# GLA heads of a two-layer trunk on one Trainium2 core: modulation steps moved behind the reads of two PSUM banks

## The chip, the cores and the metric

The program runs on 1 core of one Trainium2 chip. The metric is the time of one execution on the device, in microseconds, as the median of several runs. The core has five engines that take their instructions in order, each from a queue of its own: TensorE (PE; its weight loads are listed as PEld), VectorE (DVE), ScalarE (ACT), GpSimd (POOL) and SyncE (SP), which here only issues DMA transfers. Engines wait for one another through semaphores. Matmuls write to PSUM, eight banks called b0 to b7; everything else lies in SBUF, in slots of a fixed size.

## The reference

A trunk of two layers on one sequence of 1024 tokens with 1024 features, in float32. Each layer norms its input, modulates it by a shift and a scale that are computed from a conditioning vector c, runs a token mixer, adds the result with a gate, and does the same with a SwiGLU channel mixer. Layer 0 mixes by forgetting attention, layer 1 by gated linear attention (GLA). The parts that matter here:

```python
mod = c_act @ ada_w[i] + ada_b[i]                       # c_act = silu(c): 1024 x 6144 per layer
sh1, sc1, g1, sh2, sc2, g2 = jnp.split(mod, N_MOD, axis=-1)
...
q, k, v, r, a_lr = jnp.split(h @ w_in, [...])           # GLA: 4 heads, q and k 128 wide, v and r 256
log_alpha = log_sigmoid(a_lr @ w_a2 + b_a) / 16
b = cumsum of log_alpha within a chunk
q_in, k_in = q * exp(b), k * exp(-b)
A = tril(q_in @ k_in^T);  o_intra = A @ v
k_dec = k * exp(b_last - b);  kv = k_dec^T @ v          # state update per chunk
o = o_intra + q_in @ state;  o = norm(o) * g_o * silu(r)
```

## The kernel before

Float32 products are made of three matmuls each, on a high and a low part of both operands (mm3, lines 305 to 307; the parts are made by split, lines 174 and 175: ScalarE casts the high part, VectorE subtracts it to get the low one). The program goes through layer 0, then GLA, then the second layer's FFN. Projections read the modulated input h1 as 8 feature tiles of 128 by 1024 tokens, in two halves of 512 tokens; one half of one projection (proj) is 24 matmuls of 512 columns into one PSUM bank.

GLA runs head by head. For a head h, gate_body makes the decay factors by exponentials (ei, b16, t2). head_front then projects k (bank gk, two halves) and q (bank gqp, two halves). VectorE reads each gk bank twice, into gy = k times ei (from which kih and kil are split) and into t2 = k times its decay; it reads each gqp bank twice, into q times ei and q times b16, both split (gq..h, gq..l). head_back makes the masked products (at, L2177, ahl), the state updates (kd, kv, S_t) and the output (go), and is woven with r_proj, the projection of r (gr). gv_body projects v for the next head. The projections of gk, gqp, gr and gv take their banks in turn from one ring of three, so that a projection can start only when the bank that was used three turns before it has been read. In head 2 the first r projection takes the bank of gk's second half.

Between these parts the program also computes the modulation of layer 1. That is work for VectorE and SyncE: ada_w is read in steps of 32 * 2 rows (ada_load, L442: four transfers of 64 KB, into one of two raw buffers in turn), and a step is two instructions on VectorE (L503 or L505), each of which multiplies 256 columns by a value of c and adds them to an accumulator. A step's load can be issued only when the step two before it has been computed, since it goes into the same buffer. In names of tiles, the accumulator and the first raw buffer lie in one slot (an instruction reads ad_s only: first buffer) and the second in another (an instruction reads a second ad_s, after c: second buffer).

The call ada1(5.1) gives these steps time at fixed places of the program: the class Pace adds 5.1 to an account and runs the next pieces of a step as long as the account is not negative; a step is worth 3.6 there (ADA_A and ADA_B). The calls stand in gv_body, r_proj and head_front. The order in which the program is written is not the order on an engine: a scheduler takes the instructions in program order as its priority and places them by a timeline of its own, so that an instruction written later can come earlier on its engine.

## Time and profile before

| what | value |
|---|---|
| median of 3 runs | 2354.34 us (2350.84 to 2356.11) |
| the profiled execution | 2352.71 us |
| its span, first to last instruction | 2351.0 us |
| mean granted clock of TensorE | 0.996 |
| GLA heads, about | 1290 to 1640 us of the span |

The profile is one execution, recorded by the hardware. Its page gives busy time per engine, the chain of work that ended last and the costliest groups of instructions. In a row of the order of time the columns are: start in us from the span's start, duration in us, engine, line of the kernel, operation, output<-inputs by name (numbers left out), sizes, count, and in brackets how long the engine had been idle before and what ended that. Durations of matmuls overlap, since they are pipelined: the distance between two starts tells how fast TensorE goes. In the list of waits a row is: engine, tile and line that waited, what it waited for, us in total, how many times, the longest.

### The profile page before, as it was taken

The page shows a single profiled execution, that of the slowest core. Times are in us where ns is not written, and L with a number is a line of the kernel's source. Part 1 is how long each engine was busy: PE and PEld are TensorE (multiplying, and loading weights), DVE is VectorE, ACT ScalarE, POOL GpSimd, SP SyncE. Part 2 cuts the span into 40 slices and gives each one's busy share as a digit, 9 for nine tenths or more (in the row PEclk, how much of TensorE's full clock was granted, in tenths as well). Part 3 has the DMA queues.
Part 4 walks back from the last instruction along what each step waited for, and adds up shares of the span by engine and source line. Part 5 has one row for each costly group of instructions (what it writes and reads, how often), then busy time and mean ns, then how long its engine had stood idle before and what let it go on. Part 6 is the DMA issues. An engine that isn't in the chain of part 4 may idle for free. (4 is left out here: it accounts for less than half of the span.)

```text
span 2351.0 us, 35555 instructions
## 1 busy us (share of the span) xinstructions
PE 2327.1 (99%) x12168; PEld 1981.4 (84%) x12168; DVE 1780.7 (76%) x2947; ACT 1121.9 (48%) x2166; POOL 1139.3 (48%) x1005
## 2 busy tenths in 40 slices
PE   8999999999999999999999999999999999999999
PEld 7888888888888888888888898898888888888888
DVE  6578787886688888886787665568787777876887
ACT  6666566665453333344334644345544333345236
POOL 1334444533355656664563431335456666664651
PEclk8999999999999999999999999999999999999999
DMA  8423343332435545458774443455434544458674
GB/s 263 149 85 109 104 122 95 122 126 99 129 101 178 188 157 172 156 180 305 261 255 156 143 127 90 140 179 170 140 111 158 176 149 159 139 189 299 238 262 142
DMA packets 349614, 383.38 MB, mean 163 GB/s; under 512 B 25372, under 2 KB 286648, under 8 KB 349432
## 3 DMA queue, kind: packets, MB, share of 16 engines
q1 hardware_dynamic: 349432, 381.11, 49.3%
q8 instruction: 96, 1.57, 0.3%
q14 instruction: 86, 0.70, 0.1%
HBM read 279.76 MB, written 101.25 MB: 162 GB/s over the span
## 5 line engine op out<-in xcount | busy, mean ns | idle before, releaser
L174 ACT CAST o_s<-xv_s 128x512 fp32r<-128x512 f32 (+1 forms) x392 | 236.4, 610 | 340.2 <-PE p_b L307 257.2
L175 DVE TENSOR_TENSOR o_s<-xv_s,o_s 128x512 fp32r<-128x512 f32 (+1 forms) x392 | 336.5, 863 | 43.7 <-ACT o_s L174 43.0
L307 PE MATMUL p_b<-B,o_s 128*128 128x512 f32 x608 | 236.0, 389 | 0.0
L306 PE MATMUL p_b<-B,o_s 128*128 128x512 f32 x608 | 235.9, 389 | 0.0
L305 PE MATMUL p_b<-B,o_s 128*128 128x512 f32 x608 | 235.4, 390 | 0.0
L1293 POOL TENSOR_SCALAR lp_s<-lp_s,st 128x128 f32<-128x128 f32 (+7 forms) x128 | 96.9, 761 | 247.9 <-DVE st L1292 229.0
L940 POOL TENSOR_TENSOR ex_s<-xv_s,xv_s 128x512 f32<-128x512 f32 (+1 forms) x64 | 94.8, 1481 | 239.8 <-DMA xv_s<-in_ffn_w_in_dram 121.9
L305 PE MATMUL p_b<-T,o_s 128*128 128x512 f32 x480 | 186.8, 389 | 0.0
L306 PE MATMUL p_b<-T,o_s 128*128 128x512 f32 x480 | 186.7, 389 | 0.0
L307 PE MATMUL p_b<-T,o_s 128*128 128x512 f32 x480 | 181.2, 389 | 0.0
L307 PEld LDWEIGHTS p_b<-B,o_s 128*128 128x128 f32 x608 | 114.1, 188 | 23.9
L305 PEld LDWEIGHTS p_b<-B,o_s 128*128 128x128 f32 x608 | 114.1, 188 | 23.7 <-DVE x L1659 0.2
L306 PEld LDWEIGHTS p_b<-B,o_s 128*128 128x128 f32 x608 | 114.1, 188 | 23.5
L1291 ACT ACTIVATE lp_s<-lp_s,st 128x128 f32<-128x128 f32 (+7 forms) x128 | 99.3, 776 | 57.9 <-DVE st L1287 56.5
L942 POOL TENSOR_TENSOR xv_s<-ex_s,xv_s 128x512 f32<-128x512 f32 (+1 forms) x64 | 93.8, 1466 | 60.6 <-DVE o_s L175 57.7
L1659 DVE TENSOR_TENSOR ex_s<-ex_s,p_b 128x512 f32<-128x512 f32 x140 | 94.2, 681 | 38.0 <-PE p_b L307 37.8
L174 ACT CAST pt_s<-t_b 128x512 fp32r<-128x512 f32 (+1 forms) x160 | 79.7, 547 | 73.5 <-PE t_b L1313 72.9
L952 POOL TENSOR_TENSOR xv_s<-xv_s,xv_s 128x512 f32<-128x512 f32 x48 | 65.5, 1364 | 92.3 <-issue 50.4
L175 DVE TENSOR_TENSOR pt_s<-t_b,pt_s 128x512 fp32r<-128x512 f32 (+1 forms) x160 | 96.2, 630 | 15.9 <-ACT pt_s L174 15.4
L246 POOL TENSOR_TENSOR w_l_s<-w__s,w_h_s 128x256 fp32r<-128x256 f32 x90 | 69.4, 800 | 77.1 <-ACT w_h_s L242 59.2
L307 PEld LDWEIGHTS p_b<-T,o_s 128*128 128x128 f32 x480 | 90.1, 188 | 18.7
L306 PEld LDWEIGHTS p_b<-T,o_s 128*128 128x128 f32 x480 | 90.1, 188 | 18.7
(1527 smaller groups left out, 7409.5 us busy)
## 6 DMA issues: line engine op xcount, KB each, us to landing
xv_s<-in_ffn_w_in_dram SPq DMA_DIRECT2D x176, 256.0 KB, 3.3
hid_B<-x SPq DMA_DIRECT2D x66, 512.0 KB, 2.8
ad_s<-in_ada_w_dram SPq DMA_DIRECT2D x384, 64.0 KB, 2.4
hid_T<-x SPq DMA_DIRECT2D x44, 512.0 KB, 2.9
xv_s<-in_ffn_w_out_dram SPq DMA_DIRECT2D x88, 256.0 KB, 3.5
ada_s<-in_ada_w_dram SPq DMA_DIRECT2D x96, 128.0 KB, 2.8
T2o<-hid_T SPq DMA_DIRECT2D x22, 512.0 KB, 7.5
T1o<-hid_T SPq DMA_DIRECT2D x22, 512.0 KB, 6.2
```

The lines of the kernel that those rows point to most:

```text
L174: nc.scalar.copy(hi, src)
L175: nc.vector.tensor_sub(lo, src, hi.bitcast(F32))
L246: (nc.gpsimd if i < 3 else nc.vector).tensor_sub(lo[:, cs], rw[:, cs], hi[:, cs].bitcast(F32))
L305: nc.tensor.matmul(ps, ah, bh, start=start, stop=False, skip_group_check=chain)
L306: nc.tensor.matmul(ps, ah, bl, start=False, stop=False, skip_group_check=chain)
L307: nc.tensor.matmul(ps, al, bh, start=False, stop=stop, skip_group_check=chain)
L940: nc.gpsimd.tensor_add(s1, a21, a22)
L942: nc.gpsimd.tensor_sub(a11, s1, a11)
L952: nc.gpsimd.tensor_sub(r[A12], r[A12], r[A11])
L1291: nc.scalar.activation(lp, lp, AF.Exp, bias=mcur, scale=-1.0, accum_out=st[:, qi, 2:3])
L1293: nc.gpsimd.tensor_scalar(lp, lp, st[:, qi, 3:4], 1.0, op0=ALU.mult, op1=ALU.mult)
L1659: nc.vector.tensor_add(d, d if src is None else dest(G, src), ps)
```

## The change

In head_front two calls ada1(5.1) move. The one that stood right behind the projection of gk comes after VectorE's two multiplications that read gk's bank and after the split of the first product; the one that stood right behind the projection of gqp comes after both multiplications that read gqp's bank and after their splits. Each stands in a loop over two halves, so it is four calls a head.

```diff
             ps = pj([P, HALF], F32, f"gk{h}{hf}")
             with ExitStack() if h else tc.issue_after(z_last):
                 run(proj(ps, wk, h1, hf))
-            ada1(5.1)
             next(sums, None)
             y = yv()
             nc.vector.tensor_mul(y, ps, ei[:, cs])
             nc.vector.tensor_mul(t2[:, cs], ps, t2[:, cs])
             split(kin.hi[:, cs], kin.lo[:, cs], y)
+            ada1(5.1)
...
             ps = pj([P, HALF], F32, f"gqp{h}{hf}")
             run(proj(ps, wq, h1, hf))
-            ada1(5.1)
             next(sums, None)
             for t, f in zip(qt, (ei, b16)):
                 y = yv()
                 nc.vector.scalar_tensor_tensor(y, ps, QS, f[:, cs], op0=ALU.mult, op1=ALU.mult)
                 split(t.hi[:, cs], t.lo[:, cs], y)
+            ada1(5.1)
```

Lines 2135 to 2153 thereby move up by one: the reads of gk's bank are L2137 and L2138 before and L2136 and L2137 in the change, the reads of gqp's L2153 and L2152.

VectorE, head 2, second half of gk. The rows are a piece of the difference; gk_b_33 is that bank, ad_s_12831 alone the first raw buffer, ad_s_12832 the second:

```order
 L505 SCALAR_TENSOR_TENSOR ad_s_12831<-ad_s_12832,c_164,ad_s_12831 128x256 x2
 L505 SCALAR_TENSOR_TENSOR ad_s_12831<-ad_s_12831,c_164 128x256 x2
-L505 SCALAR_TENSOR_TENSOR ad_s_12831<-ad_s_12832,c_164,ad_s_12831 128x256 x2
-L2137 TENSOR_TENSOR gy_s_12829<-gk_b_33_14993,ei_s_9_14648 128x512
-L2138 TENSOR_TENSOR t_2_s_8_14634<-gk_b_33_14993,t_2_s_8_14634 128x512
-L505 SCALAR_TENSOR_TENSOR ad_s_12831<-ad_s_12831,c_164 128x256
+L2136 TENSOR_TENSOR gy_s_12829<-gk_b_33_14993,ei_s_9_14648 128x512
+L2137 TENSOR_TENSOR t_2_s_8_14634<-gk_b_33_14993,t_2_s_8_14634 128x512
 L246 TENSOR_TENSOR wv_0l_s_116_15145<-wv_0_s_95_15142,wv_0h_s_115_15144 128x256
```

One step (the third row) no longer stands ahead of the two reads; the step of the second row still does.

VectorE, head 1, first half of gk (bank gk_b_17) and, in the last row, the second (gk_b_18):

```order
+L2136 TENSOR_TENSOR gy_s_12829<-gk_b_17_14069,ei_s_6_13771 128x512
+L2137 TENSOR_TENSOR t_1_s_5_13757<-gk_b_17_14069,t_1_s_5_13757 128x512
+L175 TENSOR_TENSOR kil_s_4_14068<-gy_s_12829,kih_s_3_14067 128x512
 L503 TENSOR_SCALAR ad_s_12831<-ad_s_12831,c_164 128x256
 L505 SCALAR_TENSOR_TENSOR ad_s_12831<-ad_s_12831,c_164 128x256
 L505 SCALAR_TENSOR_TENSOR ad_s_12831<-ad_s_12832,c_164,ad_s_12831 128x256 x2
-L2137 TENSOR_TENSOR gy_s_12829<-gk_b_17_14069,ei_s_6_13771 128x512
-L2138 TENSOR_TENSOR t_1_s_5_13757<-gk_b_17_14069,t_1_s_5_13757 128x512
-L175 TENSOR_TENSOR kil_s_4_14068<-gy_s_12829,kih_s_3_14067 128x512
-L505 SCALAR_TENSOR_TENSOR ad_s_12831<-ad_s_12831,c_164 128x256 x2
-L505 SCALAR_TENSOR_TENSOR ad_s_12831<-ad_s_12832,c_164,ad_s_12831 128x256 x2
-L2137 TENSOR_TENSOR gy_s_12829<-gk_b_18_14120,ei_s_6_13771 128x512
```

Both steps that stood ahead of the first half's reads now stand behind them, and the next two steps have gone from ahead of the second half's.

VectorE, head 1, second half of gqp (bank gqp_b_20) and the masking L2177:

```order
 L505 SCALAR_TENSOR_TENSOR ad_s_12831<-ad_s_12832,c_164,ad_s_12831 128x256 x2
-L2153 SCALAR_TENSOR_TENSOR gy_s_12829<-gqp_b_20_14213,ei_s_6_13771 128x512
-L2153 SCALAR_TENSOR_TENSOR gy_s_12829<-gqp_b_20_14213,b_1_s_4_13756 128x512
+L505 SCALAR_TENSOR_TENSOR ad_s_12831<-ad_s_12831,c_164 128x256 x2
+L2152 SCALAR_TENSOR_TENSOR gy_s_12829<-gqp_b_20_14213,ei_s_6_13771 128x512
+L2152 SCALAR_TENSOR_TENSOR gy_s_12829<-gqp_b_20_14213,b_1_s_4_13756 128x512
 L246 TENSOR_TENSOR wv_4l_s_106_14362<-wv_4_s_90_14359,wv_4h_s_105_14361 128x256
 L175 TENSOR_TENSOR kdl_s_4_14257<-kdt_b_9_14258,kdh_s_3_14256 128x512
 L175 TENSOR_TENSOR gq10l_s_8_14171<-gy_s_12829,gq10h_s_7_14170 128x512
 L175 TENSOR_TENSOR gq11l_s_10_14173<-gy_s_12829,gq11h_s_9_14172 128x512
+L505 SCALAR_TENSOR_TENSOR ad_s_12831<-ad_s_12832,c_164,ad_s_12831 128x256
 L2177 COPY_PREDICATED atz_s_12830<-tri,at_b_4_14282 128x512
```

A step now stands directly ahead of gqp's second reads, and half a step directly ahead of the masking (the other half directly behind it).

TensorE has the same 11499 rows in both programs, and 950 lines of difference, all within the heads; its order up to the first r projection of head 2 is the same within that head.

## Prediction

> **What bounds the kernel now.** I read the page first, then the waits of TensorE (PE) in the stage that the change touches, then that stage in windows, then the order of time around the one long wait.

> ```profile
> span 2351.0 us, 35555 instructions
> PE 2327.1 (99%) x12168; PEld 1981.4 (84%) x12168; DVE 1780.7 (76%) x2947; ACT 1121.9 (48%) x2166; POOL 1139.3 (48%) x1005
> ```

> TensorE is busy for 2327.1 of 2351.0 us. No matmul is removed, so a gain can come only out of the 23.9 us in which it stands, or out of matmuls that run slowly. The four heads lie between about 1290 and 1640 us. TensorE's waits there, in total, times and longest:

> ```profile
> PE gr_b L305 <- DVE t_s L2138: 2.2, 1, 2.2
> PE oc L305 <- ACT goB L174: 0.5, 1, 0.5
> PE at_b L306 <- DVE gq10l_s L175: 0.4, 1, 0.4
> PE kdt_b L2167 <- DVE kdl_s L175: 0.2, 1, 0.2
> ```

> That is 3.3 us in all four heads, and one wait is two thirds of it: in head 2 the first r projection waits for VectorE's (DVE's) second read of gk's bank, since the bank is the same. The windows (busy us and counts by engine, granted clock, DMA share, GB/s) show what follows it.

> ```profile
> 1290.00:1500.80 210.80, 207.96 (x1288) 186.24 (x1287) 131.93 (x245) 102.73 (x242) 73.02 (x84) 1.00 0.45 129
> 1500.80:1504.20 3.40, 3.40 (x9) 2.65 (x9) 2.31 (x6) 1.45 (x6) 0.42 (x1) 0.50 0.32 96
> ```

> For 3.4 us after the wait the granted clock is 0.50. Everywhere else in the heads it is 1.00. In order of time, TensorE and then VectorE:

> ```profile
> 1498.03 0.27 PE L307 MATMUL at_b<-gq20h_s,kil_s 128*128 128x128 f32 x1
> 1500.51 0.55 PE L305 MATMUL gr_b<-h1h,w_h_s 128*128 128x512 f32 x1 [2.21 <-DVE t_s L2138]
> 1500.86 0.63 PE L306 MATMUL gr_b<-h1l,w_h_s 128*128 128x512 f32 x1
> 1501.29 0.63 PE L307 MATMUL gr_b<-h1h,w_l_s 128*128 128x512 f32 x1
> ...
> 1504.26 0.39 PE L305 MATMUL gr_b<-h1h,w_h_s 128*128 128x512 f32 x1
> 1504.49 0.40 PE L306 MATMUL gr_b<-h1l,w_h_s 128*128 128x512 f32 x1
> ```

> ```profile
> 1489.11 1.00 DVE L505 SCALAR_TENSOR_TENSOR ad_s<-ad_s,c,ad_s 128x256 f32<-128x256 f32 x2 [0.93 <-DMA ad_s<-in_ada_w_dram]
> 1496.16 1.36 DVE L505 SCALAR_TENSOR_TENSOR ad_s<-ad_s,c 128x256 f32<-128x256 f32 x2 [6.06 <-DMA ad_s<-in_ada_w_dram]
> 1497.56 1.70 DVE L505 SCALAR_TENSOR_TENSOR ad_s<-ad_s,c,ad_s 128x256 f32<-128x256 f32 x2
> 1499.18 0.68 DVE L2137 TENSOR_TENSOR gy_s<-gk_b,ei_s 128x512 f32<-128x512 f32 x1
> 1499.78 0.67 DVE L2138 TENSOR_TENSOR t_s<-gk_b,t_s 128x512 f32<-128x512 f32 x1
> 1501.89 0.48 DVE L505 SCALAR_TENSOR_TENSOR ad_s<-ad_s,c 128x256 f32<-128x256 f32 x1 [1.43 <-DMA ad_s<-in_ada_w_dram]
> ```

> VectorE takes its instructions in order. Two modulation steps (four L505) stand ahead of the read of gk's bank. The first waits 6.06 us for its weights, both are computed, and only then the bank is read, at 1499.18 and 1499.78. A step is two L505: one pair reads the first raw buffer (ad_s<-ad_s,c), the next the second (ad_s<-ad_s,c,ad_s). So a modulation step, which nobody needs before the next layer, holds up TensorE.

> **The change part by part.** Nothing is added or removed: the same L505, the same transfers, the same matmuls. In head 2 only the second of the two steps has gone behind the read; the first, with the 6.06 us wait, still stands ahead of it. (The program's order is given to a scheduler, which sets the order on each engine.)

> *The read in head 2.* It moves up by what stood between: from 1499.18 to 1497.56, 1.62 us. The r projection follows it as now (the second read ends at 1500.45, the matmul starts at 1500.51), so TensorE's idle time goes from 2.21 to 0.59 us: **-1.62**. This holds if the transfer behind the 6.06 us lands when it does now. SyncE's queue (SPq), start and length:

> ```profile
> 1484.07 3.16 SPq L442 DMA_DIRECT2D ad_s<-in_ada_w_dram  x4
> 1487.33 1.00 SPq L1002 DMA_DIRECT2D ow<-pw_s  x2
> 1488.45 0.71 SPq L227 DMA_DIRECT2D w__s<-in_gla_w_in_dram  x1
> 1489.27 16.33 SPq L442 DMA_DIRECT2D ad_s<-in_ada_w_dram  x20
> ```

> The load is the first four of the x20, behind two stores and a weight load of 512 KB each. The changed kernel has the same order on SyncE from the x4 at 1484.07 to the third step of the x20, so I take the landing as unchanged. Bounds: if it came so early that the read waits for nothing, the whole 2.21 goes; if one more step of four loads (3.16 us, the first row) stood ahead of it, the hole would be 0.59 + 3.16 = 3.75 and this term +1.54.

> *The clock.* At full clock a 512-wide matmul starts 0.23 us after the last (1504.26, 1504.49), in the slow stretch 0.43 us after (1500.86, 1501.29). Nine of them took from 1500.51 to 1504.26, 3.75 us, against 9 x 0.23 = 2.07: 1.68 us lost. No other hole of the heads, all at most 0.5 us, is followed by a lower clock, and neither is this one of 2.0 us earlier in the program:

> ```profile
> PE t_b L1313 <- POOL lp_s L1293: 2.0, 1, 2.0
> 400.00:420.00 20.00, 18.01 (x110) 15.38 (x109) 17.13 (x47) 9.04 (x22) 5.57 (x9) 1.00 0.52 151
> ```

> So 2.21 us was enough here and 2.0 there was not; 0.59 us is nearest to the holes of 0.5. I take the stretch as gone: **-1.68**, bounds 0 and -1.68.

> [...]

> *Head 1.* Here VectorE gets ahead by more. TensorE and VectorE before:

> ```profile
> 1415.51 0.33 PE L305 MATMUL at_b<-gq10h_s,kih_s 128*128 128x128 f32 x1
> 1416.24 0.33 PE L306 MATMUL at_b<-gq10l_s,kih_s 128*128 128x128 f32 x1 [0.40 <-DVE gq10l_s L175]
> 1413.20 1.01 DVE L505 SCALAR_TENSOR_TENSOR ad_s<-ad_s,c 128x256 f32<-128x256 f32 x2 [3.24 <-DMA ad_s<-in_ada_w_dram]
> 1414.12 0.68 DVE L2153 SCALAR_TENSOR_TENSOR gy_s<-gqp_b,ei_s 128x512 f32<-128x512 f32 x1
> ```

> Five steps stand ahead of gqp's first read, and the fifth waits 3.24 us for its load; TensorE then waits 0.40 us for what comes of the read. In the changed order three steps stand there, and the two that are gone include the fifth. The read comes some microseconds earlier: **-0.40**. It cannot be more, as TensorE waits for nothing else there.

> *What the moved steps meet.* They land between gqp's two halves and around the masking L2177 of heads 0 and 1; VectorE has room, 131.93 busy of 210.80 us. Their loads move with them: SyncE's queue has weight loads and the ow stores ahead of a step or two that were behind them before. TensorE's own order changes in 950 lines, all of it matmuls of the heads passing one another by a few places; I cost that at nothing, because at most 0.5 us is idle anywhere else in the heads, and the bound the other way is the slower rival below.

> *Given back.* Later TensorE waits 0.46 us for a transfer at the end of a chain over GpSimd (POOL):

> ```profile
> 1630.62 8.09 DMA og_s<-og_d
> 1638.73 0.63 ACT goB L174
> 1639.47 0.47 PE L305 MATMUL oc<-goT,ow_s 128*128 128x512 f32 x1 [0.46 <-ACT goB L174]
> 1606.28 0.69 POOL L2239 TENSOR_TENSOR gss<-gss,mhalf 128x2 f32<-128x2 f32 x1 [5.54 <-DVE gss L2238]
> 1620.70 0.69 POOL L2239 TENSOR_TENSOR gss<-gss,mhalf 128x2 f32<-128x2 f32 x1 [1.71 <-DVE gss L2238]
> ```

> If TensorE comes 3.7 us earlier (1.62 + 1.68 + 0.40), the chain must too, or the wait grows. GpSimd waits 5.54 and 1.71 us there for values that come from TensorE's own matmuls, so most of the chain moves along; at worst only the last 1.71 does, and 3.7 - 1.7 = 2.0 is given back. Bounds 0 and +2.0; nearer to 0, for the 5.54: **+0.5**.

> **The sum.** -1.62 - 1.68 - 0.40 + 0.5 = -3.2 us. The profiled execution took 2352.71 us (2351.0 of span and 1.7 around it), so it would come to 2349.5. The median of the runs shown is 2354.34, 1.63 above it; the same step from there gives the forecast, **2351.1 us**, 0.14% less.

> **The rivals.**

> [...]

> *Slower: the wait goes with the step.* In heads 0 and 1 a modulation step now stands directly ahead of the masking L2177, from which ahl is made, which TensorE needs for the go products. In head 0 before (ScalarE, then TensorE):

> ```profile
> 1350.19 0.62 ACT L174 CAST ahl_s<-atz_s 128x512 fp32r<-128x512 f32 x1 [2.16 <-DVE atz_s L2177]
> 1352.17 0.28 PE L305 MATMUL go_b<-gvt_s,ahl_s 128*128 128x256 f32 x1
> ```

> The cast ends at 1350.81 and is needed at 1352.17: 1.36 us to spare. If the step there waits for its load as long as the longest here, 6.06 us, TensorE stands for 4.70 us, and with a slow stretch like that of head 2 (1.68) the cost is 6.4; less the 3.7 of the gain, +2.7: 2357.0. It is slower than before from a wait of about 1.36 + 3.7 - 1.68 = 3.4 us on. For it: SyncE's queue puts 512 KB transfers ahead of these loads. Against it: fewer steps stand ahead of the masking than before, VectorE is there earlier in head 1 by up to the 3.24 us, and a wait that falls on a VectorE that is early costs nothing.

> *The change does not do what it says.* The load in head 2 lands later by the 1.62 us gained, since steps and loads have moved everywhere upstream; hole and slow stretch stay: 2354.3. For it: the queue's bulk transfers, not the order on VectorE, set 1496.16. Against it: the order on SyncE ahead of that load is the same.

> **How the numbers follow.** Forecast 0.50, hole only 0.20, slower 0.17, nothing 0.13. About 0.2%, 4.7 us, is what a measurement of this kernel can tell from no change; the three runs before span 5.3 us (2350.84 to 2356.11), so a median can lie some 2.6 us off. Faster by over 4.7 needs the forecast and 1.5 us of luck, or all at its best (1.62 + 0.59 + 1.68 + 0.40 + 0.46 = 4.75): some 0.33 of the forecast, a little of the others, 0.20. Slower by over 4.7 needs the second rival with a wait in both heads, or with bad luck: half of it and a little of the rest, 0.12. The rest, 0.68, is within. The range: all at its best, 2349.6, less 2.6, 2347; up to the slower rival, 2357.

> **What would show it.** The first r projection of head 2 waits some 0.6 us for the read of gk's bank (now L2137), and the granted clock is 1.00 right through the heads; the wait of at_b for gq10l is gone; oc's wait for goB is between 0.5 and 2.5; L505 still waits some 6 us for its load ahead of gk's second read in head 2. Wrong would be: a wait of go for ahl, or of any matmul of the heads, of over 1 us; a slow stretch; or a load that lands later than before against TensorE's place.

## The result, and the profile after

The changed kernel takes 2349.36 us (median of 22 runs, 2346.71 to 2352.11), the kernel before 2354.17 us beside it (22 runs, 2348.87 to 2356.58). The two medians are 4.8 us apart. The ratio of the runs is 0.9982, with a 95% interval from 0.9975 to 0.9988: 4.2 us faster, between 2.8 and 5.9. Differences below are worked out from ratios where nothing else is said. A second comparison (e8 below) gave 0.9987 (0.9978 to 0.9996), 3.1 us. The forecast was a step of -3.2 us, to 2351.1 with a range from 2347 to 2357.

The profiled execution of the changed kernel took 2349.75 us, with a span of 2348.0 (the one of before took 2352.71, with a span of 2351.0). TensorE's waits in the heads and the first output products (1280 to 1660 us): in total, times, longest. This is the answer to the list in the prediction.

```profile
PE oc L305 <- DVE x L2386: 1.8, 2, 1.6
```

The waits of gr_b, of at_b and of kdt_b are gone. oc now waits for another thing than before, and longer. Apart from oc, the only wait listed there is one of 0.2 us. The clock is 1.00 through the heads (busy us and counts by engine, granted clock, DMA share, GB/s):

```profile
1290.00:1640.00 350.00, 348.23 (x2112) 310.10 (x2111) 232.79 (x414) 173.94 (x401) 129.92 (x132) 1.00 0.47 143
```

In order of time, VectorE and then TensorE around the second read of gk's bank in head 2:

```profile
1495.73 1.00 DVE L505 SCALAR_TENSOR_TENSOR ad_s<-ad_s,c 128x256 f32<-128x256 f32 x2 [5.43 <-DMA ad_s<-in_ada_w_dram]
1496.65 0.68 DVE L2136 TENSOR_TENSOR gy_s<-gk_b,ei_s 128x512 f32<-128x512 f32 x1
1497.26 0.68 DVE L2137 TENSOR_TENSOR t_s<-gk_b,t_s 128x512 f32<-128x512 f32 x1
1498.36 0.28 PE L307 MATMUL at_b<-gq20h_s,kil_s 128*128 128x128 f32 x1
1498.47 0.44 PE L305 MATMUL gr_b<-h1h,w_h_s 128*128 128x512 f32 x1
```

One step (a pair of L505, 1.00 us) stands ahead of the read instead of two. The read ends at 1497.94, TensorE needs the bank at 1498.47, and waits for nothing.

How long do the heads take? The same two groups of matmuls give it in both kernels, from the first gk to the last go (shortest, median and longest duration in ns, first and last start in us, before and after):

```profile
L305 PE MATMUL gk_b<-h1h,w_h_s x64: 387/389/396, 1321.8 to 1578.3; 128*128 128x512 f32 x64
L305 PE MATMUL go_b<-gvt_s,ahl_s x32: 277/283/387, 1352.2 to 1626.4; 128*128 128x256 f32 x32
```

```profile
L305 PE MATMUL gk_b<-h1h,w_h_s x64: 389/389/475, 1323.8 to 1575.6; 128*128 128x512 f32 x64
L305 PE MATMUL go_b<-gvt_s,ahl_s x32: 276/283/364, 1354.9 to 1623.0; 128*128 128x256 f32 x32
```

That is 304.6 us before and 299.2 after, 5.4 less. It is more than the 3.0 us between the two spans, since the changed kernel's execution came into the heads 2.0 us later (1323.8 against 1321.8; the edit does not touch what lies ahead of them), and it gave 1.1 us back at oc (0.46 to 1.56); the remaining 0.7 us was won behind it. Ahead of the heads the changed kernel's clock was at 0.50 from 60.85 to 67.68 and from 415.84 to 419.25 us, where the execution of before had 1.00. So single executions differ by things that are not the change. This is why the last part compares these stage times, and not the spans.

### The profile page after: what moved, and what is told of

Same layout as the page of the kernel before. It is cut to its first block, busy times and chain, and to the rows that moved or that the text cites. A ratio compares the mean times of both kernels' runs of the same rounds, so it can differ in the third digit from the quotient of the medians.

```text
span 2348.0 us, 35560 instructions
## 1 busy us (share of the span) xinstructions
PE 2327.2 (99%) x12168; PEld 1984.9 (85%) x12168; DVE 1778.5 (76%) x2947; ACT 1123.2 (48%) x2166; POOL 1141.2 (49%) x1005
## 3 DMA queue, kind: packets, MB, share of 16 engines
q8 instruction: 96, 1.57, 0.3%
## 4 chain that ended last, share of the span: by engine, by line
PE 88%; DVE 4%; DMA 3%; issue 1%; ACT 1%; POOL 1%; SPq 1%; DVEq 0%; POOLq 0%; ACTq 0%
PE p_b L305 16%; PE p_b L307 16%; PE p_b L306 16%; PE o_b L1327 2%; PE t_b L1313 2%; PE qk_b L305 2%; PE qk_b L306 2%; PE qk_b L307 2%; PE vps_b L307 1%; PE vps_b L305 1%; PE vps_b L306 1%; PE gv_b L305 1%; PE gv_b L307 1%; PE gv_b L306 1%; PE gr_b L305 1%
## 5 line engine op out<-in xcount | busy, mean ns | idle before, releaser
L174 ACT CAST o_s<-xv_s 128x512 fp32r<-128x512 f32 (+1 forms) x392 | 236.3, 610 | 340.1 <-PE p_b L307 254.3
L175 DVE TENSOR_TENSOR o_s<-xv_s,o_s 128x512 fp32r<-128x512 f32 (+1 forms) x392 | 335.6, 861 | 43.2 <-ACT o_s L174 42.6
L307 PE MATMUL p_b<-B,o_s 128*128 128x512 f32 x608 | 236.0, 389 | 0.0
L306 PE MATMUL p_b<-B,o_s 128*128 128x512 f32 x608 | 235.9, 389 | 0.0
L305 PE MATMUL p_b<-B,o_s 128*128 128x512 f32 x608 | 235.4, 390 | 0.0
L1293 POOL TENSOR_SCALAR lp_s<-lp_s,st 128x128 f32<-128x128 f32 (+7 forms) x128 | 98.0, 769 | 246.0 <-DVE st L1292 227.0
L305 PE MATMUL p_b<-T,o_s 128*128 128x512 f32 x480 | 186.8, 389 | 0.0
L306 PE MATMUL p_b<-T,o_s 128*128 128x512 f32 x480 | 186.7, 389 | 0.0
L307 PE MATMUL p_b<-T,o_s 128*128 128x512 f32 x480 | 181.2, 389 | 0.0
L307 PEld LDWEIGHTS p_b<-B,o_s 128*128 128x128 f32 x608 | 114.1, 188 | 23.9
L305 PEld LDWEIGHTS p_b<-B,o_s 128*128 128x128 f32 x608 | 114.1, 188 | 23.7 <-DVE x L1659 0.2
L306 PEld LDWEIGHTS p_b<-B,o_s 128*128 128x128 f32 x608 | 114.1, 188 | 23.5
L174 ACT CAST pt_s<-t_b 128x512 fp32r<-128x512 f32 (+1 forms) x160 | 79.7, 547 | 73.6 <-PE t_b L1313 73.0
L246 POOL TENSOR_TENSOR w_l_s<-w__s,w_h_s 128x256 fp32r<-128x256 f32 x90 | 69.3, 799 | 85.9 <-ACT w_h_s L242 67.9
L175 DVE TENSOR_TENSOR pt_s<-t_b,pt_s 128x512 fp32r<-128x512 f32 (+1 forms) x160 | 96.2, 630 | 15.9 <-ACT pt_s L174 15.4
L307 PEld LDWEIGHTS p_b<-T,o_s 128*128 128x128 f32 x480 | 90.1, 188 | 18.7
L306 PEld LDWEIGHTS p_b<-T,o_s 128*128 128x128 f32 x480 | 90.1, 188 | 18.7
```

The source lines that it names most:

```text
L174: nc.scalar.copy(hi, src)
L175: nc.vector.tensor_sub(lo, src, hi.bitcast(F32))
L246: (nc.gpsimd if i < 3 else nc.vector).tensor_sub(lo[:, cs], rw[:, cs], hi[:, cs].bitcast(F32))
L305: nc.tensor.matmul(ps, ah, bh, start=start, stop=False, skip_group_check=chain)
L306: nc.tensor.matmul(ps, ah, bl, start=False, stop=False, skip_group_check=chain)
L307: nc.tensor.matmul(ps, al, bh, start=False, stop=stop, skip_group_check=chain)
```

## The experiments

**Where does the gain come from?** My theory: from one place, the read of gk's second bank in head 2. The rival: from the new order of all heads. e1 moves the calls in head 2 alone, e2 everywhere but there.

The edit of e1 at gk's call (e2 has the two conditions exchanged; gqp's call is treated alike). In e1, e2 and e5 the moved call of gk stands behind ScalarE's exponentials, in the change ahead of them; no run tests this difference by itself.

```diff
-            ada1(5.1)
+            if not (h == 2):
+                ada1(5.1)
...
             nc.scalar.activation(b16[:, cs], b16[:, cs], AF.Exp, scale=-1.0 / 16)
+            if h == 2:
+                ada1(5.1)
```

> The four calls are moved in head 2 alone; heads 0, 1 and 3 are as before. Theory (one place): TensorE's wait for the second read of gk's bank in head 2 (2.2 us) and the slow stretch behind it (about 1.7 us) are the gain, and oc gives back up to 1.5: 2.5 to 4.2 us faster than the kernel before, no wait of gr in head 2, at_b's wait of 0.4 in head 1 still there. Rival (spread): the gain is the sum of many small shifts in the order of all heads, so head 2 alone brings 1 us or less.

> The calls are moved in heads 0, 1 and 3, and stand where they stood in head 2. Theory (one place): gr in head 2 waits some 2 us for gk's bank again, with the slow stretch behind it; only at_b's 0.4 us in head 1 is won: 0 to 1 us faster than the kernel before. Rival (spread): 3 us or more faster with the wait in head 2 still there.

Measured: e1 0.9989 (0.9980 to 0.9998), 2.6 us faster; e2 0.9995 (0.9986 to 1.0003), 1.2 us, not told from nothing. VectorE and TensorE of e1, TensorE of e2:

```profile
1499.39 1.36 DVE L505 SCALAR_TENSOR_TENSOR ad_s<-ad_s,c 128x256 f32<-128x256 f32 x2 [5.74 <-DMA ad_s<-in_ada_w_dram]
1501.28 0.68 DVE L2139 TENSOR_TENSOR t_s<-gk_b,t_s 128x512 f32<-128x512 f32 x1
1502.01 0.50 PE L305 MATMUL gr_b<-h1h,w_h_s 128*128 128x512 f32 x1 [0.63 <-DVE t_s L2139]
```

```profile
1498.19 0.49 PE L305 MATMUL gr_b<-h1h,w_h_s 128*128 128x512 f32 x1 [2.09 <-DVE t_s L2139]
```

e1 looks like the prediction's picture of head 2: a pair of 1.36 us, the reads, and a wait of 0.63 us (forecast 0.59). That it agrees to 0.04 us is partly luck, since its load landed 3.2 us later than in the kernel before and TensorE came 3.1 us later too. Against its expectation gr does wait. e2 keeps the wait of 2.09, but without the expected slow stretch behind it. By the middle values the larger part comes from head 2, and both parts together make about the whole. The two intervals (0.5 to 4.7 us and -0.7 to 3.3) overlap, though, so the times alone do not show how the gain is shared. What e1 leaves are head 1's waits, of 0.2 us each.

**Which of the two pairs of calls?** e5 moves gk's calls in all heads, e6 gqp's.

The edit of e5; e6 has the other half of the change in its place (gqp's call, ahead of the t loop before, behind it now):

```diff
-            ada1(5.1)
+            if not (True):
+                ada1(5.1)
             next(sums, None)
...
             nc.scalar.activation(b16[:, cs], b16[:, cs], AF.Exp, scale=-1.0 / 16)
+            if True:
+                ada1(5.1)
```

> Only gk's two calls are moved, in all heads; gqp's stand where they stood. Theory (gk's read in head 2): the second step is behind the read, so gr's wait in head 2 falls from 2.2 to at most 0.6 us: 2 to 4 us faster than the kernel before. Rival (gqp): gqp's calls carry the gain, and this kernel is within 1 us of the one before.

> Only gqp's two calls are moved, in all heads; gk's stand where they stood, and two steps stand ahead of gk's second read in head 2 as in the kernel before. Theory (gk's read in head 2): gr waits 2.0 to 2.2 us there; only head 1's 0.4 to 1 us is won, so within 1 us of the kernel before or of the kernel with heads 0, 1 and 3 alone moved (1.3 us faster). Rival (gqp): 3 us or more faster. On the clock: if the wait of 2 us by itself brings the slow stretch, its profile has half clock for 3.4 us just behind the wait, as the kernel before had; if not, there is none, as where heads 0, 1 and 3 alone were moved (2.1 us of waiting, clock 1.00).

Measured: e5 0.9995 (0.9987 to 1.0004), e6 0.9993 (0.9984 to 1.0002). By their times neither is told from the kernel before or from the other. e5's 1.2 us miss the 2 to 4 that were expected, while its gr waits for nothing, as expected; e6's 1.6 us are within what was expected, while its gr waits 0.60 us and not 2.0 to 2.2. Their profiles say more. VectorE and TensorE of e5 in heads 2 and 1, then of e6 in head 2:

```profile
1497.60 0.69 DVE L2138 TENSOR_TENSOR gy_s<-gk_b,ei_s 128x512 f32<-128x512 f32 x1 [1.15 <-PE gk_b L307]
1422.53 0.66 PE L2170 MATMUL kdt_b<-ident,t_s 128*128 128x128 f32 x4 [0.59 <-DVE kdl_s L175]
```

```profile
1497.13 1.01 DVE L505 SCALAR_TENSOR_TENSOR ad_s<-ad_s,c 128x256 f32<-128x256 f32 x2 [5.37 <-DMA ad_s<-in_ada_w_dram]
1498.79 1.36 DVE L505 SCALAR_TENSOR_TENSOR ad_s<-ad_s,c,ad_s 128x256 f32<-128x256 f32 x2 [0.66 <-DMA ad_s<-in_ada_w_dram]
1500.68 0.68 DVE L2138 TENSOR_TENSOR t_s<-gk_b,t_s 128x512 f32<-128x512 f32 x1
1501.41 0.50 PE L305 MATMUL gr_b<-h1h,w_h_s 128*128 128x512 f32 x1 [0.60 <-DVE t_s L2138]
```

In e5 VectorE is so early that it waits for TensorE's gk (1.15 us), and a wait of kdt in head 1 has grown from 0.23 to 0.59. In e6 both steps still stand ahead of the read, as before the change, and yet gr waits 0.60 us and not 2.2. Theory and rival fall here in part: the number of steps ahead of the read is not all that sets the wait.

**What sets it.** The kernel before was profiled two more times (e7, e11), and the changed one once more (e8).

> The kernel before, profiled once more. Theory (the wait brings the slow stretch): gr waits 2.2 us in head 2 again and 3.4 us at half clock follow. Rival (chance): the same wait, and no slow stretch behind it, or one elsewhere.

> The changed kernel again, beside the next two on one chip: 3 to 5 us faster than the kernel before (as first measured), and oc waits 1.6 us for L2386 as it did.

> The kernel before, profiled a third time. In the profiles so far all slow stretches of one execution begin a whole number of steps of 3.413 us apart, and the step ahead of a slow one shows TensorE busy for 1.1 to 1.7 us, that ahead of a full one for 1.7 us or more. Theory (fixed steps): count steps from any slow stretch of this execution; where the wait of gr (2.2 us, head 2) leaves TensorE busy for under 1.6 us in one step, the next 3.4 us are at half clock; where the wait is shared by two steps that both show over 1.8 us, none follows; the same for the wait of t_b near 412. Rival (chance, or the wait's length alone): no such rule; a step with under 1.6 us goes unpunished, or a slow stretch follows a step with over 1.8 us.

e8's interval is given above. TensorE of e7; VectorE of e11, whose TensorE does not wait for the bank at all; VectorE and TensorE of e8:

```profile
1502.72 0.50 PE L305 MATMUL gr_b<-h1h,w_h_s 128*128 128x512 f32 x1 [2.16 <-DVE t_s L2138]
```

```profile
1494.30 1.00 DVE L505 SCALAR_TENSOR_TENSOR ad_s<-ad_s,c 128x256 f32<-128x256 f32 x2 [5.04 <-DMA ad_s<-in_ada_w_dram]
1495.72 1.01 DVE L505 SCALAR_TENSOR_TENSOR ad_s<-ad_s,c,ad_s 128x256 f32<-128x256 f32 x2 [0.42 <-DMA ad_s<-in_ada_w_dram]
1497.24 0.68 DVE L2138 TENSOR_TENSOR t_s<-gk_b,t_s 128x512 f32<-128x512 f32 x1
```

```profile
1498.14 1.50 DVE L505 SCALAR_TENSOR_TENSOR ad_s<-ad_s,c 128x256 f32<-128x256 f32 x2 [5.81 <-DMA ad_s<-in_ada_w_dram]
1500.17 0.67 DVE L2137 TENSOR_TENSOR t_s<-gk_b,t_s 128x512 f32<-128x512 f32 x1
1500.90 0.50 PE L305 MATMUL gr_b<-h1h,w_h_s 128*128 128x512 f32 x1 [0.41 <-DVE t_s L2137]
```

The same kernel waits 2.2 us in two executions and not at all in the third. One subtraction accounts for all of these. The *path* runs from the landing of the first step's load to the end of the second read. The *margin* runs from that landing to the end of the at products, when TensorE wants the bank:

| execution | steps ahead | path us | margin us | path - margin | wait of gr us |
|---|---|---|---|---|---|
| before | 2 | 1496.16 to 1500.45: 4.29 | 2.14 | 2.15 | 2.21 |
| before, third (e11) | 2 | 1494.30 to 1497.92: 3.62 | 4.00 | -0.38 | none |
| gqp only (e6) | 2 | 1497.13 to 1501.36: 4.23 | 3.68 | 0.55 | 0.60 |
| head 2 only (e1) | 1 | 1499.39 to 1501.96: 2.57 | 1.99 | 0.58 | 0.63 |
| changed | 1 | 1495.73 to 1497.94: 2.21 | 2.91 | -0.70 | none |
| changed, again (e8) | 1 | 1498.14 to 1500.84: 2.70 | 2.35 | 0.35 | 0.41 |

The other profiles fit as well. With two steps, e2, e7, e10 and e12 have paths of 4.64, 4.44, 4.29 and 4.99 us and margins of 2.61, 2.34, 2.05 and 2.21, and each waits what is left, to within 0.1 us. With one step, e4 and e9 have paths of 2.21 and margins of 2.79 and 2.64, and do not wait. (e3 has extra reads, and in e5 VectorE waits for gk itself, so the subtraction does not apply there.)

The change takes 1.4 to 1.7 us off the path (3.62 to 2.21 where the pairs run at 1.00 us, 4.29 to 2.57 where they take 1.36 and more); that is the 1.62 of the prediction. The order does not fix the path alone: with two steps it lies between 3.62 and 4.99 us, with one between 2.21 and 2.70, by how fast the pairs run and by a wait of up to 0.66 us for the second step's load. The margin is set by when the load lands against TensorE's place, and lies between 2.0 and 4.0 us by the run and by the order upstream. With two steps gr waits in six of seven profiles, 0.60 to 2.84 us; with one it waits 0.63 us at most in six (e3 left out). Read so, the change makes a kernel robust that was sometimes as good by luck: e11's execution took 2347.96 us, e7's 2354.81.

Why the pairs take 1.00 or 1.36 us and more can be read from the traces. In the 14 profiles all 2500 instructions of L505 that had no GpSimd instruction beside them took 0.46 to 0.49 us each. Every one of over 0.50 us had GpSimd at work beside it for 45% of its time or more; some with GpSimd beside them were not slowed. In the kernel before, GpSimd's splits of wv (L246) begin at 1496.44, within the first pair; in the changed kernel they begin at 1496.77, behind it.

**The clock.** The prediction gave 1.68 us to a stretch at half clock behind the wait. e3 tried to bring wait and stretch back in the changed kernel, by four extra reads of gk's bank.

```diff
-            nc.vector.tensor_mul(y, ps, ei[:, cs])
+            for _ in range(5 if (h, hf) == (2, 1) else 1):
+                nc.vector.tensor_mul(y, ps, ei[:, cs])
```

> The changed kernel, with the first multiplication that reads gk's second bank in head 2 done five times over instead of once (the same values each time): four extra VectorE multiplications of about 0.61 us ahead of the read that frees the bank. Theory (hole and clock): the read ends 2.4 to 3.2 us later than in the changed kernel (where it ended 0.5 us ahead of the need), gr waits 2 to 2.7 us, and a stretch of 3.4 us at half clock follows it: 3.5 to 4.5 us slower than the changed kernel, about the time of the kernel before. Rival (hole alone): the slow stretch has nothing to do with this hole and does not come back: 2 to 2.7 us slower than the changed kernel.

Measured: 1.0011 (1.0002 to 1.0020), 2356.61 us, 7.3 us above the changed kernel's 2349.36 by the medians and 6.8 by the ratios. Both theories miss it. TensorE of e3:

```profile
1499.32 0.38 PE L305 MATMUL go_b<-gvt_s,ahl_s 128*128 128x256 f32 x1 [1.47 <-ACT ahl_s L174]
1501.03 0.50 PE L305 MATMUL gr_b<-h1h,w_h_s 128*128 128x512 f32 x1 [0.81 <-DVE t_s L2138]
```

The extra reads did not make one long wait. They held up the masking and the split of ahl behind them, so go waited for ahl (1.47 us) and for the state, gr 0.81: what the slower rival had feared, brought about by the extra reads. A slow stretch did follow, from 1501.92 on, but this run does not tell what brings it.

The repeats do. The kernel before again had a wait of 2.16 us in e7, and no slow stretch behind it, but one at 415.8. e2 had 2.09 us and none. e10 (a kernel with the same heads, below) had two, at 415.42 and 1504.27 to be exact, 1088.85 us or 319 times 3.4133 apart; in the changed kernel's profiled execution those at 60.85 and 415.84 start 354.99 us apart, 104 times 3.4133. So the slow stretches of these executions start on fixed steps of 3.41 us. In the windows that are cut on these steps, the step ahead decides: e10, then e7, then the changed kernel near the wait of t_b for lp_s (1.94 us there), then the kernel before at the same place.

```profile
1500.85:1504.26 3.41, 1.12 (x7) 0.89 (x7) 2.51 (x4) 1.36 (x5) 3.40 (x5) 1.00 0.28 75
1504.26:1507.67 3.41, 3.41 (x10) 2.63 (x9) 2.73 (x7) 1.44 (x4) 0.00 (x0) 0.50 0.29 84
```

```profile
1497.84:1501.25 3.41, 2.73 (x21) 2.38 (x19) 2.92 (x4) 2.18 (x4) 2.54 (x4) 1.00 0.16 44
1501.25:1504.66 3.41, 1.94 (x8) 1.61 (x9) 1.86 (x5) 2.27 (x6) 2.19 (x3) 1.00 0.36 106
1504.66:1508.07 3.41, 3.41 (x16) 2.81 (x15) 3.41 (x8) 1.59 (x3) 0.00 (x0) 1.00 0.27 80
```

```profile
412.43:415.84 3.41, 1.66 (x11) 1.43 (x12) 3.35 (x11) 1.06 (x2) 0.95 (x1) 1.00 0.03 9
415.84:419.25 3.41, 3.41 (x16) 3.02 (x15) 2.92 (x12) 2.42 (x7) 1.35 (x2) 0.50 0.91 288
```

```profile
408.55:411.96 3.41, 1.74 (x12) 1.38 (x10) 2.40 (x7) 2.44 (x6) 0.69 (x1) 1.00 0.58 163
411.96:415.37 3.41, 3.10 (x22) 2.79 (x23) 3.30 (x9) 1.28 (x3) 0.26 (x1) 1.00 0.27 73
```

Where a wait of some 2 us lies within one step, TensorE is busy for 1.12 us of 3.41 and the next step is granted 0.50. Where two steps share it, they show 2.73 and 1.94, and the clock stays at 1.00. The length of the wait alone does not decide: t_b waits 1.80 us in e7 and 1.94 in the changed kernel, and the slow stretch comes; it waits 1.99 in the kernel before, and none comes.

The edge lies between 1.66 (slow) and 1.74 (full), about half of the step. This is the count of all steps between 75 and 2330 us of the 14 executions: those with TensorE busy for 1.66 us or less are eight, and all were followed by a slow one. Of the 15 with 1.74 to 2.0 us, one was followed by a slow one (e3, 1.79), 14 were not.

Some slow stretches do not fit this count. One (e1, at 655.9) follows a step that shows 3.14 us busy. And near 61 us, 11 of the 14 executions have half clock for one or two steps, behind steps that show 3.3 us or more, as here in the changed kernel:

```profile
58.67 1.84 PE L595 MATMUL mp_b<-cact,adas_s 128*128 128x1 f32 x16
57.44:60.85 3.41, 3.33 (x26) 2.85 (x24) 3.05 (x5) 1.43 (x2) 0.00 (x0) 1.00 1.05 407
60.85:64.26 3.41, 3.41 (x15) 3.02 (x14) 0.33 (x2) 1.23 (x2) 0.00 (x0) 0.50 1.05 408
```

In all twelve, 1.5 to 2.0 us of that busy time are products one column wide. Without these products the twelve steps show 1.45 to 1.80 us, and the three executions without a slow stretch near 61 us show 1.95 or more there. From these fifteen steps I estimate that such products do not count in full, and that the edge, counted without them, lies between 1.73 and 1.80. No run tried this by itself, and it does not account for the second slow step near 61 us, where there is one.

The rule was made from the runs up to e10. e11 (above) and e12 (e2's kernel again) were its test:

> The calls moved in heads 0, 1 and 3 alone, profiled again; gr waits some 2.1 us in head 2. Theory (fixed steps): as for the run beside it, a step of 3.413 us with TensorE busy for under 1.6 us is followed by 3.4 us at half clock, one with over 1.8 us is not. Rival (chance): no such rule. oc's wait for L2386: 1.6 us where no slow stretch came in head 2, under 1 us where one came.

e12's step near 1500, and the next:

```profile
1499.11:1502.52 3.41, 0.87 (x4) 0.74 (x5) 2.59 (x5) 1.49 (x5) 2.56 (x4) 1.00 0.31 96
1502.52:1505.93 3.41, 3.41 (x10) 2.63 (x9) 3.41 (x8) 2.09 (x6) 0.00 (x0) 0.50 0.28 91
```

e12 waited 2.84 us, nearly all of it within one step, which shows 0.87 us busy, and the slow stretch came; its step at 413.67 shows 1.99, and none came. e11 has no step under 2.0 between 75 and 2330 us and no slow stretch between 60 and 2300 us. Its gr did not wait, so it does not put the rule to a hard test. Both agree with it.

**The wait that came at oc.** VectorE, GpSimd and TensorE of the changed kernel there:

```profile
1632.52 3.48 DVE L175 TENSOR_TENSOR goT<-og_s,goT 128x512 fp32r<-128x512 f32 x2
1635.92 0.74 DVE L2386 SCALAR_TENSOR_TENSOR x<-oc,modc,x 128x512 f32<-128x512 f32 x1
1632.14 1.61 POOL L2440 TENSOR_TENSOR og_s<-og_s,og_s 128x512 f32<-128x512 f32 x1 [1.90 <-DVE goB L175]
1633.70 1.75 POOL L2439 TENSOR_TENSOR og_s<-og_s,og_s 128x512 f32<-128x512 f32 x1
1636.81 0.47 PE L305 MATMUL oc<-goT,ow_s 128*128 128x512 f32 x1 [1.56 <-DVE x L2386]
```

TensorE needs the bank that the addition to x_0 (L2386) frees. Ahead of that addition stand the splits of T1, pairs 2 and 3, which only the oe products need. With GpSimd at work beside them they take 3.48 us for two. In the kernel before, GpSimd waited for a transfer meanwhile, and they took 2.37:

```profile
1636.29 2.37 DVE L175 TENSOR_TENSOR goT<-og_s,goT 128x512 fp32r<-128x512 f32 x2
1638.77 1.28 POOL L2439 TENSOR_TENSOR og_s<-og_s,og_s 128x512 f32<-128x512 f32 x1 [1.27 <-DMA og_s<-og_d]
```

e4 and e9 put them behind the addition in the changed kernel, e10 in the kernel before.

```diff
-        for j in (2, 3):
-            a = og_t[j]
-            with behind_all():
-                nc.vector.tensor_sub(a[:, h0_], og_t[4 + j][:, h0_], a[:, h1_])
-                ob_split("T1", j, a[:, h0_])
...
                     out_add(2 * g, 0, pa[g])
+                    for j in (2, 3) if g == 0 else ():
+                        a = og_t[j]
+                        with behind_all(), tc.issue_after(last_of("D")):
+                            nc.vector.tensor_sub(a[:, h0_], og_t[4 + j][:, h0_], a[:, h1_])
+                            ob_split("T1", j, a[:, h0_])
```

> The changed kernel, and the subtractions and splits that make T1 of pairs 2 and 3 (needed only by the oe products) put behind the addition L2386 to x_0 that frees oc's first bank. Theory: the new wait of oc for that addition (1.6 us at 1636.8 of the changed kernel) is gone and stays gone: 1 to 1.6 us faster than the changed kernel, some 6 us faster than before. Rival (the next wait): TensorE meets the og_s load behind goB or the masked-out tail of the head 1 to 2 us later and gives it all back: the time of the changed kernel within 0.5 us.

> The changed kernel with T1 of pairs 2 and 3 put behind the addition to x_0, again. Theory: oc's wait of 1.6 us is gone, so 1 to 1.6 us less than the changed kernel beside it. Rival (the next wait): within 0.5 us of it.

> The kernel before, with T1 of pairs 2 and 3 put behind the addition to x_0, and nothing else. Theory (oc's wait of 1.6 us was there before and was hidden only in the one execution in which TensorE came late by the slow stretch): 1 to 1.6 us faster than the kernel before. Rival (the wait is new with the change, given back for the gain): oc waits 0.5 us in the kernel before, so it gains 0.5 us at most. gr waits 2.2 us in head 2 as before in both.

Measured: e4 0.9974 (0.9964 to 0.9985), 2348.09 us; e9 0.9983 (0.9974 to 0.9992), 2348.10 us beside 2350.07 for the changed kernel on the same chip (e8). e10 1.0000 (0.9991 to 1.0009). The addition in e4:

```profile
1632.71 0.74 DVE L2386 SCALAR_TENSOR_TENSOR x<-oc,modc,x 128x512 f32<-128x512 f32 x1
```

It runs 3.2 us earlier, though this execution left the heads 1.4 us later than the changed kernel's (last go at 1624.4 against 1623.0), and oc waits for nothing there. In e9 a later oc product still waits 0.51 us for such an addition. The wait did not simply move on: by the medians the kernel gains another 1.3 and 2.0 us, by the ratios 1.9 and 0.9, each time in the same direction. The intervals overlap, so this gain is likely and not shown. By its medians this is the fastest version here. In the kernel before the edit shows no gain that can be told, and its interval of 2.1 us either way holds both expectations, so e10 decides nothing by its time. What it leaves open e7 settles: the unchanged kernel waits 1.56 us at oc for L2386 there, just as the changed one does, so the wait is not new. Its size goes with the two T1 splits: 3.47 or 3.48 us where oc waited 1.55 to 1.58 (e7, the changed kernel, e8, and also e1, e2, e5 and e6), 2.37 or 2.38 where it waited 0.46 to 0.49 (before, e11, e12). My expectation for e12, that a slow stretch in head 2 hides the wait, came true by its number and is wrong by its reason: e11 had no slow stretch and waited 0.47. What differs is how long GpSimd waits for the transfer of its og_s meanwhile (0.70 to 1.27 us in before, e11 and e12, 0.40 at most in the seven others), and so how much of the time it works beside VectorE.

## Why the prediction was right, point by point

The direction was right, and so was the largest single place, head 2. The size was right too, in part by luck (see the sum below). Over four executions with the old heads (before, e7, e11, e10) the stage time is 304.6, 303.3, 300.5 and 305.0 us, mean 303.4. Over four with the new heads (after, e8, e4, e9; the further edit of e4 and e9 lies behind the heads) it is 299.2, 299.8, 299.0 and 298.8, mean 299.2. That is 4.2 us less. At oc some 0.7 comes back (0.46, 1.56, 0.47 in before, e7 and e11 against 1.56, 1.56 in the changed kernel and e8), which leaves 3.5, between the two timed comparisons.

*The read in head 2, -1.62.* Right on average, though the account was too simple. The step taken out of the path is 1.62 us long in the execution that I read. The weak point was "I take the landing as unchanged": the landing against TensorE's place differs by 2 us from one execution to another. The mean wait went from 1.67 us (2.21, 2.16, none, 2.29) to 0.10 (none, 0.41, none, none), so -1.57. That this comes within 0.05 us of the forecast is luck, with four executions on either side. The single profiled execution after had no wait, where I had forecast 0.6.

*The clock, -1.68.* That a slow stretch follows from the hole was right, the size was that of one execution taken for all. The stretch followed the wait in two of the four executions with the old heads, so it was worth about 0.84 on average (an estimate: half of the 1.68). The hole was read as a length against a threshold (2.21 slow, 2.0 not); what counts, by the count above, is how much of one fixed step it empties.

*Head 1, -0.40, "it cannot be more".* Mis-sized. Idle time as the profile lists it was less here than what the stop cost: 0.40 us is listed for at_b, and from start to start the stop was 1415.51 to 1416.24, 0.73 us, where the changed kernel has

```profile
1417.38 0.22 PE L305 MATMUL at_b<-gq10h_s,kih_s 128*128 128x128 f32 x1
1417.44 0.27 PE L306 MATMUL at_b<-gq10l_s,kih_s 128*128 128x128 f32 x1
```

so some 0.6 to 0.7, and kdt's wait beside it 0.4 where 0.2 was listed:

```profile
1420.11 0.40 PE L306 MATMUL gr_b<-h1l,w_h_s 128*128 128x512 f32 x1
1420.73 0.66 PE L2167 MATMUL kdt_b<-ident,t_s 128*128 128x128 f32 x4 [0.23 <-DVE kdl_s L175]
```

(0.62 from start to start, against 0.23 for a 512-wide matmul.) Together 1.0. Two comparisons give what the change does beside the wait in head 2. e11, which had no such wait and no slow stretch, is 1.3 us longer in the heads than the changed kernel. e7 (303.3) is 2.2 us longer than e2 (301.1, its heads 0, 1 and 3 changed); both have that wait, of 2.16 and 2.09 us, and no slow stretch in the heads, so some 2.1 are left. Each is a pair of single executions. The prediction was weak here: it priced the other holes at what the list of waits says, and of the 1.3 to 2.1 us only the 1.0 of head 1 is placed.

*Given back, +0.5.* The size was near (0.7, from three executions against two, which is few), the mechanism wrong. The wait of 1.56 us lies within the 0.5 to 2.5 that were named as a sign, but it is for another instruction. Not the chain over GpSimd and og_s delays TensorE, but VectorE's order at x_0's addition; GpSimd matters by the splits ahead of it, which took 2.37 us where it waited 1.27 us for its transfer (the kernel before) and 3.48 where it worked on beside them (the changed kernel), and the wait comes without the change too (e7).

*The sum.* With what was measured it is -1.57 - 0.84 - 1.3 + 0.7 = -3.0 us, or -3.8 with 2.1 in the place of 1.3, against -3.2 forecast and -3.5 from the stage times. That the forecast came so near is in part luck: the clock was priced 0.84 too high, and what the change does outside that wait 0.9 or more too low, and the two errors cancel.

*The rivals.* What the chances call "hole only", a gain at the wait without one at the clock, happens in executions where no slow stretch would have come. "Does not do what it says" did not come true: the wait is under 0.7 us in every profile with one step ahead (e3, with its extra reads, left out). "Slower: the wait goes with the step", the "second rival" of the chances, did not come about. In head 0 of the changed kernel, VectorE, ScalarE and TensorE:

```profile
1351.46 0.47 DVE L505 SCALAR_TENSOR_TENSOR ad_s<-ad_s,c,ad_s 128x256 f32<-128x256 f32 x1
1351.86 0.73 DVE L2177 COPY_PREDICATED atz_s<-tri,at_b 128x512 f32<-128x512 int32 x1
1352.62 0.62 ACT L174 CAST ahl_s<-atz_s 128x512 fp32r<-128x512 f32 x1 [2.56 <-DVE atz_s L2177]
1354.87 0.28 PE L305 MATMUL go_b<-gvt_s,ahl_s 128*128 128x256 f32 x1
```

The step directly ahead of the masking L2177 waits for nothing and takes 0.47, and ahl is ready 1.63 us before go needs it. A masking that is held up did cost time in e3, where go waited 1.47 us.

*The range.* The scatter of some 5 us on either kernel, which I had taken as measurement, is in part the kernel's own. The first gk starts between 1321.3 us (e2) and 1326.0 (e6) with nothing edited ahead of it, slow stretches near 61 and 415 us come or do not, and in head 2 the hole is there or not. The three executions without the stretch near 61 us (before, e2, e11) are the earliest at the first gk, 1321.3 to 1322.1 us.

## What to carry to other kernels

A wait of an in-order engine for a transfer is best priced as a path minus a margin: the path is what the order sets, apart from the pace of the engines, and an edit can shorten, the margin is the landing and differs from one execution to the next (2.1 and 4.0 us in two of the same kernel here), so take more than one profile before a hole is called a constant. Work that nobody waits for goes behind the read that frees a PSUM bank, and once that is done, look for the next such read (here the addition to x_0, behind splits that nobody needed yet). Price a stop of TensorE from start to start, not by the listed idle time (0.73 against 0.40 us at at_b).
